# Contraction-outermost order behind the norms, late squares, and SSD decay masks as scaled ScalarE copies

## The chip, the cores and the metric

The kernel runs on one core of a Trainium2 chip: TensorE (PE, matrix products), VectorE (DVE), ScalarE (ACT), GpSimd (POOL) and SyncE (SP, which issues the DMAs). The metric is the device time of one launch in microseconds (us), taken as the median of several runs.

## The reference

The function is one inference step of a two-layer recurrent trunk of width 1024 over 592 columns (16 meta tokens, 512 prompt tokens, 8 samples of 8 tokens). Layer 0 mixes with SSD heads (16 heads of 64) and RG-LRU blocks, layer 1 with GLA and HGRN heads. Each layer ends twice in a layer norm:

```
h = LN(alpha*h + mixer(h));  h = LN(alpha*h + relu(h @ w1)^2 @ w2)
LN(x): mu = mean(x); var = mean((x - mu)^2); (x - mu) * rsqrt(var + eps) * g + b

# SSD, per chunk of q tokens and per head
xbc = silu(b + sum(full[:, t:t+L] * w[t] for t in range(4)))     # causal convolution of width 4
b = cumsum(log_a);  decay = exp(where(t >= s, b_t - b_s, -inf))  # q x q, per head
y_intra = (c_t . b_s) * decay @ (x*dt);  y_inter = (c_t . S) * exp(b_t)
S = S * exp(b_last) + b^T (x * dt * exp(b_last - b))
```

All of it is float32; new recurrent states are outputs too.

## The kernel before, in words

Activations lie with the 1024 features in eight tiles of 128 partitions and with the 592 columns along the free dimension, in two halves of 296 (288 in the later stages, where the meta columns are dropped). A product of float32 quality is three fp32r matmuls (high·high, high·low, low·high), so one output tile of one half is 24 matmuls of 128x128x296: eight contraction steps k times three. Weights arrive by DMA as units of 128x1024 (`raw`); ACT casts the high part (L126) and DVE subtracts the low part (L127). Five units of prepared weights and five PSUM banks `pm` are in rotation (three more banks, `px`, serve small products).

A task (`Task`, L276) is one weight unit over both halves; `mm` (L176) runs its 24 matmuls of one half, and `consume` empties the bank. `run(..., by_half=True)` goes through all tasks' first halves, then through their second halves. `later` holds work that `mm` issues after a given k. The order of every engine comes from a scheduler that looks at the whole program with its own costs; each engine then runs its list strictly in order.

**The norms** (`Norm`, L395) stand behind each output projection and each MLP. While the last product is made, each finished residual tile is added to a running sum (L444) and its square (ACT, L446) to a running sum of squares (DVE, L447). `finishing` (L457) sends both sums through PE with a matrix of ones (L463 mean, L465 variance), and then, tile by tile, DVE and POOL subtract the mean (L478, L480), DVE scales (L494), ACT rounds to the high part of the next input `h` (L495) and DVE makes the low part (L496). For half 0 the statistics are issued inside the first product of half 1, after step `FIK`; for half 1 they come after it. The next stage's first block of products (in the MLP L648, `w1` tasks; in the odd mixer a small product `lr` at L247 and q, k, v) starts on half 0 while half 1 is being finished. Its banks are emptied by ACT (L588 in the MLP, L1366 and L1381 in the odd mixer).

**The SSD part** works in two groups of four pairs of heads (`pair`, L832), in stages between which other work is woven. A pair needs the log decays (high and low part, `lah` and `lal`, 128 x 16 heads per chunk) times a triangular mask: `rr` (2 x 4 chunks x 2 heads x 128) and `rx` (2 x 2 x 80). POOL makes them with two 128x1024 products (L843) and two of 128x160 (L845). PE sums them (L879, L884), ACT takes the exponential (L881, L885), DVE multiplies it by the scores (L886, L887). Then come the state products: DVE L897 writes `yi0` from a `px` bank, which PE's L918 waits for; L911 updates the running state `S`, which L925 reads; POOL's L899 scales the samples' states `sin`. Between these, `conv_task` (L687) makes the next inputs: ACT empties the bank (L697 to L702), DVE does the first tap (L706, tensor_scalar) and the next taps (L708 twice, L781 once), ACT the silu (L783), DVE L787 the product. The same `conv_task` serves the RG-LRU blocks, whose PE product is L1067.

Of the kernel before, what the change touches and what calls it, by code (L numbers as in the profile page):

```python
# [8 lines left out]
F32 = mybir.dt.float32  # L9
# [5 lines left out]
P = 128  # L15
# [8 lines left out]
NPM = 5  # L24
NB = 5
SHK = 5
FIK = 3
FINY = (2, 4, 6)
SUBP = (1, 3, 5, 7)
KS = 8 - NB  # L30
# [41 lines left out]
def _trunk(ctx, tc, nc, I, O):  # L72
# [12 lines left out]
    def pm():  # L85
        return pmp.tile([P, 512], F32, tag="pm", name="pm")
# [83 lines left out]
    def next_unit():  # L170
        u = state["use"]
        state["use"] += 1
        prep_to(u + 1 + LOOK)
        return prepped.pop(u)
# [25 lines left out]
    def flush():  # L200
        while pending:
            pending.pop(0)()
# [66 lines left out]
    def drain():  # L269
        while active or later:  # L270
            for k in sorted(later):
                for fn in later.pop(k):
                    fn()
            weave()

    class Task:  # L276
# [6 lines left out]
        def half(self, i):  # L283
# [8 lines left out]
            flush()  # L292
            weave()

    def run(tasks, by_half=False, after=None):
        if by_half:
            for i in range(2):
                for t in tasks:
                    t.half(i)
                if after:  # L300
                    after(i)
        else:
            for t in tasks:
                t.half(0)
                t.half(1)
# [89 lines left out]
    class Norm:  # L395
# [3 lines left out]
        def __init__(self, new, rs, halves, gname, bname, layer, final=False):  # L399
            self.rs, self.halves, self.final = rs, halves, final  # L400
            self.gname, self.bname, self.layer = gname, bname, layer
            self.new = new

        def shift(self):

# [25 lines left out]
        def add(self, k, i):  # L431

            c0, c1 = self.halves[i]
            r = self.rs[k][:, c0:c1]
            if k == KS:
                V.tensor_tensor(r, r, self.c[:, c0:c1], OP.subtract)
            s, ss = self.s[:, c0:c1], self.ss[:, c0:c1]
            if k == 0:
                A.activation(ss, r, AF.Square)
                return  # L440
            if k == 1:
                G.tensor_tensor(s, self.rs[0][:, c0:c1], r, OP.add)
            else:
                (V if k == KT - 1 else G).tensor_tensor(s, s, r, OP.add)  # L444
            q = self.t[k % 2][:, c0:c1]
            A.activation(q, r, AF.Square)  # L446
            V.tensor_tensor(ss, ss, q, OP.add)  # L447

        def finish(self, i, dst):
            if i == 0:  # L450
                later.setdefault(FIK, []).append(lambda: step(self.finishing(i, dst)))
            else:
                drain()
                for _ in self.finishing(i, dst):
                    pass

        def finishing(self, i, dst):  # L457
            c0, c1 = self.halves[i]
            n = c1 - c0
            gname, bname, layer = self.gname, self.bname, self.layer  # L460
            s, ss, rstd, m2 = (t[:, c0:c1] for t in (self.s, self.ss, self.rstd, self.m2))
            mu = px()[:, :n]
            PE.matmul(mu, ones, s, start=True, stop=True)  # L463
            var = px()[:, :n]
            PE.matmul(var, ones, ss, start=True, stop=True)  # L465
            A.activation(m2, mu, AF.Square, scale=1.0 / D)
            if ln_set:
                tc.keep_in_program_order(A.preload_act_table_set("natural_log_exp_and_others"))
                ln_set.clear()
            V.scalar_tensor_tensor(rstd, var, 1.0 / D, m2, OP.mult, OP.subtract)  # L470
            A.activation(rstd, rstd, AF.Ln, bias=LN_EPS)
            A.activation(rstd, rstd, AF.Exp, scale=-0.5)
            mn = self.t[0][:, c0:c1]
            A.activation(mn, mu, AF.Copy, scale=1.0 / D)
            for k in range(KT):
                r = self.rs[k][:, c0:c1]
                if k not in SUBP:
                    V.tensor_tensor(r, r, mn, OP.subtract)  # L478
                else:
                    G.tensor_tensor(r, r, mn, OP.subtract)  # L480
            for k in range(KT):
                if k in FINY:
                    yield
                r = self.rs[k][:, c0:c1]
                gain, b = vc(gname, layer * 8 + k), vc(bname, layer * 8 + k)
                if self.final:
                    if k % 2 == 0:
                        y = act_tile(hp, "h").bitcast(F32)[:, :, 0:n]
                    V.scalar_tensor_tensor(r, r, gain, rstd, OP.mult, OP.mult)
                    A.activation(y[:, k % 2], r, AF.Identity, bias=b)  # L490
                    if k % 2:
                        nc.sync.dma_start(O["yT"][:, k - 1:k + 1, c0 - NM:c1 - NM], y)
                else:
                    V.scalar_tensor_tensor(r, r, gain, rstd, OP.mult, OP.mult)  # L494
                    A.activation(dst[k][:, 0, c0:c1], r, AF.Identity, bias=b)  # L495
                    V.scalar_tensor_tensor(dst[k][:, 1, c0:c1], r, b, dst[k][:, 0, c0:c1].bitcast(F32),  # L496
                                           OP.add, OP.subtract)
# [49 lines left out]
    def mlp(H, layer, halves, last, keep=None):  # L547
# [3 lines left out]
        with ExitStack() as st:  # L551
# [93 lines left out]
                        G.tensor_scalar(rs[k], rs[k], vc("ln2b", layer * 8 + k), None, OP.add)  # L645
                        G.dma_start(keep[:, k], rs[k])

            run([w1(0, f) for f in W1_ORDER[:4]], by_half=True)  # L648
            for k, f in enumerate(W1_ORDER[4:]):
                run([w1(0, f)])  # L650
                residual(2 * k)
# [24 lines left out]
    def even_mixer(H, g):  # L676
# [10 lines left out]
        def conv_task(i, w, b, done):  # L687
# [3 lines left out]
            def consume(p, c0, c1, half):  # L691
# [11 lines left out]
                G.tensor_copy(pconv[:, i], t[:, 528:531])  # L703
                G.tensor_copy(sconv[:, i], s8(t)[:, :, 8:11])
                acc = cp.tile([P, PW], F32, tag="acc", name="acc")
                V.tensor_scalar(acc[:, 0:OW], t[:, 0:OW], w(0), b, OP.mult, OP.add)  # L706
                for k in (1, 2):
                    V.scalar_tensor_tensor(acc[:, 0:OW], t[:, k:k + OW], w(k), acc[:, 0:OW], OP.mult, OP.add)  # L708
                done(t, acc)
# [122 lines left out]
        def pair(j, xs, zs, gs):  # L832
# [6 lines left out]
            nc.sync.dma_start(sin, I["sst"][j])  # L839
            rr = s1.tile([P, 2, 4, 2, P], F32R, tag="rr", name="rr")  # L840
            rx = s1.tile([P, 2, 2, 80], F32R, tag="rx", name="rx")
            for i, l in enumerate((lah.bitcast(F32), lal.bitcast(F32))):
                G.tensor_tensor(rr[:, i], l[:, 1:5, hh].unsqueeze(3).to_broadcast([P, 4, 2, P]),  # L843
                                umask[:, None, None, :].to_broadcast([P, 4, 2, P]), OP.mult)
                G.tensor_tensor(rx[:, i], l[:, 0, hh].unsqueeze(2).to_broadcast([P, 2, 80]),  # L845
                                uxmask[:, None, 0:80].to_broadcast([P, 2, 80]), OP.mult)
            xr = s1.tile([P, 2, 3, 40], F32, tag="xr", name="xr")
            A.copy(xr, xs[:, 0:80].rearrange("p (h c) -> p h c", h=2).unsqueeze(2).to_broadcast([P, 2, 3, 40]))
            yield
            xd = s2.tile([P, 5, 2, 64], F32, tag="xd", name="xd")  # L850
            xdte = s1.tile([P, 4, 2, 64], F32, tag="xdte", name="xdte")
            xst = s1.tile([P, 2, 2, 64], F32, tag="xst", name="xst")
# [268 lines left out]
    def odd_mixer(H, g):  # L1121
# [278 lines left out]
        for h in range(4):  # L1400
            q, k, v0, v1 = (g(n) for n in ("q", "k", "v", "v"))
            tasks = [copy_task(q, TAIL), copy_task(k, FULL), copy_task(v0, FULL), copy_task(v1, FULL)]
            if h == 0:
                run([Task(H, FULL, lr_consume, small=wsr[:, 1])] + tasks[0:NB], by_half=True)
                run(tasks[NB:])
            else:
                run(tasks)
            z = [g("zs"), g("zs")]
# [214 lines left out]
```

## Time and profile before

| | us |
|---|---|
| median of 3 runs (lowest, highest) | 1928.42 (1928.1, 1928.71) |
| profiled execution | 1926.06 |
| its span, first to last instruction | 1924.3 |
| mean granted TensorE clock in the span | 0.987 of full |
| PE busy | 1858.2 (97%) |
| DVE busy | 1297.1 (67%) |
| ACT busy | 886.0 (46%) |
| POOL busy | 417.2 (22%) |

PE is busy for 97% of the span, so the time can fall only where PE waits or where its granted clock is low. The profile names for each wait of PE the instruction that ended it.

### The profile page before, as it was taken

What the parts mean: (1) busy time and instruction counts of PE and PEld (TensorE: products, weight loads), DVE (VectorE), ACT (ScalarE), POOL (GpSimd) and SP (SyncE); (2) the same over time, 40 slices, a digit from 0 to 9 for tenths busy, and PEclk for the clock granted to TensorE, in tenths of its full rate; (3) what the DMA queues carried; (4) which work ended last, traced back from release to release, by engine and by line L of the source; (5) the groups of instructions that cost most, each with busy time, mean ns of one, the idle gap of its engine ahead of it and who ended that gap; (6) DMA issues with size and microseconds to landing.
All of it is one profiled execution on the core that took longest, in us unless ns stands there. A gap on an engine that the chain in (4) does not pass through costs nothing.

```text
span 1924.3 us, 33593 instructions
## 1 busy us (share of the span) xinstructions
PE 1858.2 (97%) x13854; PEld 1819.0 (95%) x13854; DVE 1297.1 (67%) x2035; ACT 886.0 (46%) x1550; POOL 417.2 (22%) x435
## 2 busy tenths in 40 slices
PE   8998899999999999998999999999999999999996
PEld 8998799899999999998999999999999999999996
DVE  7997766877975756549645465665755976666647
ACT  5333246623644444324644455665732653534333
POOL 2554432214100000035422222221203200000024
PEclk9999899999999999999999999999999999999998
DMA  6232221421213131322332233223231214141311
GB/s 205 91 114 72 75 100 47 132 88 47 87 56 120 46 127 48 122 76 72 132 113 104 100 104 106 84 90 102 91 126 56 77 56 132 46 131 55 122 55 50
DMA packets 68761, 175.97 MB, mean 91 GB/s; under 512 B 6624, under 2 KB 30304, under 8 KB 67456
## 3 DMA queue, kind: packets, MB, share of 16 engines
q1 hardware_dynamic: 67968, 171.40, 26.5%
q8 instruction: 109, 1.79, 0.4%
q0 software_dynamic: 640, 2.43, 0.4%
q14 instruction: 44, 0.36, 0.1%
HBM read 154.54 MB, written 19.25 MB: 90 GB/s over the span
## 4 chain that ended last, share of the span: by engine, by line
PE 80%; DVE 13%; ACT 3%; issue 3%; POOL 0%; DMA 0%; SPq 0%; ACTq 0%; DVEq 0%; POOLq 0%
PE pm L182 55%; PE pm L195 14%; DVE w L127 1%; DVE r L424 1%; DVE h L496 1%; DVE r L494 1%; PE px L1326 1%; DVE r L478 1%; PE px L1337 1%; PE px L1336 1%; PE px L1067 1%; DVE lnq L447 1%; DVE acc L708 1%; PE px L925 1%; DVE ln L447 1%
## 5 line engine op out<-in xcount | busy, mean ns | idle before, releaser
L182 PE MATMUL pm<-h,w 128*128 128x296 f32 (+2 forms) x8256 | 1178.2, 301 | 11.0 <-ACT h L308 5.4
L182 PEld LDWEIGHTS pm<-h,w 128*128 128x128 f32 x8256 | 1132.6, 189 | 22.6 <-ACT h L308 5.4
L127 DVE TENSOR_TENSOR w<-raw,w 128x1024 fp32r<-128x1024 f32 (+1 forms) x300 | 369.7, 1233 | 165.1 <-ACT w L126 164.5
L126 ACT CAST w<-raw 128x1024 fp32r<-128x1024 f32 (+1 forms) x300 | 304.2, 1015 | 301.6 <-PE pm L195 152.2
L195 PE MATMUL pm<-ff,w 128*128 128x296 f32 (+1 forms) x2016 | 273.3, 297 | 0.0
L195 PEld LDWEIGHTS pm<-ff,w 128*128 128x128 f32 x2016 | 271.9, 188 | 0.1
L620 POOL TENSOR_TENSOR sq<-sq 128x296 f32<-128x296 f32 (+1 forms) x32 | 21.5, 674 | 651.4 <-ACT sq L618 651.4
L182 PE MATMUL pm<-m,w 128*128 128x296 f32 (+1 forms) x768 | 108.2, 304 | 0.0
L182 PE MATMUL pm<-ff,w 128*128 128x296 f32 (+1 forms) x768 | 108.0, 303 | 0.0
L182 PEld LDWEIGHTS pm<-m,w 128*128 128x128 f32 x768 | 106.8, 194 | 0.8 <-issue 0.3
L182 PEld LDWEIGHTS pm<-ff,w 128*128 128x128 f32 x768 | 106.6, 193 | 0.8 <-issue 0.3
L607 DVE TENSOR_TENSOR ff<-sq,ff 128x888 fp32r<-128x888 f32 (+3 forms) x48 | 58.4, 1221 | 42.1 <-ACT ff L606 42.1
L588 ACT ACTIVATE sq<-pm 128x296 f32<-128x296 f32 (+1 forms) x96 | 37.9, 414 | 87.0 <-PE pm L182 66.0
L606 ACT CAST ff<-sq 128x888 fp32r<-128x888 f32 (+3 forms) x48 | 50.3, 1050 | 39.6 <-DVE sq L601 38.9
L1361 POOL TENSOR_TENSOR o<-o,zs 128x576 f32<-128x576 f32 x16 | 31.3, 1967 | 148.7 <-DVE o L1360 148.7
L1280 POOL TENSOR_TENSOR sin<-sin,ebl 128x1024 f32<-128x1024 f32 (+1 forms) x12 | 35.8, 2980 | 106.1 <-issue 101.2
L211 DVE TENSOR_TENSOR r<-r,pm 128x296 f32<-128x296 f32 (+1 forms) x96 | 43.5, 453 | 18.6 <-PE pm L195 18.0
L589 ACT ACTIVATE sq<-sq 128x296 f32<-128x296 f32 (+1 forms) x96 | 41.2, 450 | 0.8
L1366 ACT COPY v<-pm 128x296 f32<-128x296 f32 x32 | 12.9, 405 | 58.6 <-PE pm L182 58.6
L214 DVE TENSOR_TENSOR r<-r,pm 128x296 f32<-128x296 f32 (+1 forms) x72 | 32.6, 452 | 10.2 <-PE pm L195 10.2
L618 ACT ACTIVATE sq<-pm 128x296 f32<-128x296 f32 (+1 forms) x32 | 13.0, 414 | 56.8 <-PE pm L182 53.8
L495 ACT ACTIVATE h<-r,vec 128x296 fp32r<-128x296 f32 (+1 forms) x48 | 23.8, 536 | 31.5 <-DVE r L494 31.5
(390 smaller groups left out, 2261.3 us busy)
## 6 DMA issues: line engine op xcount, KB each, us to landing
raw<-in_w_dram SPq DMA_DIRECT2D x252, 512.0 KB, 3.3
sin<-in_sst_dram SPq DMA_DIRECT2D x8, 512.0 KB, 3.7
out_ssd_s_dram<-sin SPq DMA_DIRECT2D x8, 512.0 KB, 3.1
sin<-in_gst_dram SPq DMA_DIRECT2D x4, 1024.0 KB, 5.7
out_gla_s_dram<-sin SPq DMA_DIRECT2D x4, 1024.0 KB, 3.9
sin<-in_hst_dram SPq DMA_DIRECT2D x8, 512.0 KB, 4.4
out_hgrn_s_dram<-sin SPq DMA_DIRECT2D x8, 512.0 KB, 3.5
xt<-in_x_dram SPq DMA_DIRECT2D x16, 148.0 KB, 4.2
```

What stands on the lines that cost most here:

```text
L126: A.copy(w[:, 0, :n], r)
L127: V.tensor_tensor(w[:, 1, :n], r, w[:, 0, :n].bitcast(F32), OP.subtract)
L182: PE.matmul(p[:, :n], w[:, a, ks], xs[k][:, b, c0:c1], start=(k == 0 and i == 0), stop=(k == KT - 1 and i == 2))
L195: PE.matmul(p[:, :n], w[:, a, ks], xs[k][:, b, :n], start=(first and k == 0 and i == 0), stop=(k == 3 and i == 2), skip_group_check=True)
L211: V.tensor_tensor(y, y, p[:, :n], OP.add)
L214: V.tensor_tensor(y, y, p[:, :n], OP.subtract)
L447: V.tensor_tensor(ss, ss, q, OP.add)
L588: A.activation(q, p, AF.Relu)
L589: A.activation(q, q, AF.Square)
L606: A.copy(t[:, 0, a:e, :n], s[:, a + 1:e + 1, :n])
L607: V.tensor_tensor(t[:, 1, a:e, :n], s[:, a + 1:e + 1, :n], t[:, 0, a:e, :n].bitcast(F32), OP.subtract)
L1280: G.tensor_tensor(sin, sin, ebl[:, 0:8].unsqueeze(2).to_broadcast([P, 8, N]), OP.mult)
```

## The change

The statistics of half 0 are issued after step 6 instead of step 3 of the first product of half 1. `together` runs several tasks with the contraction step outermost: step k of all tasks, then step k+1, and empties all banks at the end. It is used for the first four tasks behind the three norms that have a successor (four tasks on half 0, then two and two on half 1). The addition of a square to its running sum is issued one tile later. Weights of four units are asked for before the drain. The first convolution tap becomes an ACT instruction, and the masks times log decays become 20 ACT copies per pair of heads, each with a per-partition scale.

```diff
-FIK = 3
+FIK = 6
+    def together(tasks, i):
+        ps = []
+        for t in tasks:
+            if t.small is None and t.w is None:
+                t.w = next_unit()
+            ps.append(pm())
+        for k in range(KT):
+            ks = slice(k * P, (k + 1) * P)
+            for t, p in zip(tasks, ps):
+                c0, c1 = t.halves[i]
+                if t.small is not None:
+                    ops = [(p[:32], t.small[:, k, :], b) for b in range(2)]
+                else:
+                    ops = [(p, t.w[:, a, ks], b) for a, b in ((0, 0), (0, 1), (1, 0))]
+                for j, (o, w, b) in enumerate(ops):
+                    PE.matmul(o[:, :c1 - c0], w, t.xs[k][:, b, c0:c1], start=(k == 0 and j == 0),
+                              stop=(k == KT - 1 and j == len(ops) - 1))
+            for fn in later.pop(k, ()):
+                fn()
+        for t, p in zip(tasks, ps):
+            c0, c1 = t.halves[i]
+            t.consume(p[:32 if t.small is not None else P, :c1 - c0], c0, c1, i)
+            flush()
+            weave()
...
             A.activation(q, r, AF.Square)
-            V.tensor_tensor(ss, ss, q, OP.add)
+            self.add_square()
+            self.square = (ss, q)
+        def add_square(self):
+            if self.square:
+                ss, q = self.square
+                V.tensor_tensor(ss, ss, q, OP.add)
+            self.square = None
...
             else:
+                prep_to(state["use"] + 4)
                 drain()
...
         def finishing(self, i, dst):
+            self.add_square()
...
-            run([w1(0, f) for f in W1_ORDER[:4]], by_half=True)
+            ts = [w1(0, f) for f in W1_ORDER[:4]]
+            together(ts, 0)
+            together(ts[:2], 1)
+            together(ts[2:], 1)
...
-                V.tensor_scalar(acc[:, 0:OW], t[:, 0:OW], w(0), b, OP.mult, OP.add)
+                A.activation(acc[:, 0:OW], t[:, 0:OW], AF.Identity, scale=w(0), bias=b)
...
-            for i, l in enumerate((lah.bitcast(F32), lal.bitcast(F32))):
-                G.tensor_tensor(rr[:, i], l[:, 1:5, hh].unsqueeze(3).to_broadcast([P, 4, 2, P]),
-                                umask[:, None, None, :].to_broadcast([P, 4, 2, P]), OP.mult)
-                G.tensor_tensor(rx[:, i], l[:, 0, hh].unsqueeze(2).to_broadcast([P, 2, 80]),
-                                uxmask[:, None, 0:80].to_broadcast([P, 2, 80]), OP.mult)
+            def decays(m):
+                for i, l in enumerate((lah.bitcast(F32), lal.bitcast(F32))):
+                    for h in range(2):
+                        def scaled(out, mask, c):
+                            A.activation(out, mask, AF.Copy, scale=l[:, c, 2 * j + h:2 * j + h + 1])
+                        if m == 2:
+                            scaled(rx[:, i, h], uxmask[:, 0:80], 0)
+                        else:
+                            for c in (2 * m, 2 * m + 1):
+                                scaled(rr[:, i, c, h], umask, c + 1)
+            decays(0)
...
             yield
+            decays(1)
+            decays(2)
...
             if h == 0:
-                run([Task(H, FULL, lr_consume, small=wsr[:, 1])] + tasks[0:NB], by_half=True)
-                run(tasks[NB:])
+                ts = [Task(H, FULL, lr_consume, small=wsr[:, 1])] + tasks
+                together(ts[:4], 0)
+                ts[4].half(0)
+                together(ts[:2], 1)
+                together(ts[2:4], 1)
+                ts[4].half(1)
```

In the changed file the lines below L291 lie further down: L843 becomes L888, L899 becomes L950, L463 and L465 become L500 and L502, L783 becomes L823, and so on.

POOL's list in the sixth pair of heads (pair 5), before: `lah` and `lal` are the log decays, `msk` the triangular mask.

```order
L868 TENSOR_TENSOR xdte<-xd,ex 128x512
L703 COPY pconv<-pad 128x3
L843 TENSOR_TENSOR rr<-lah,msk 128x1024
L845 TENSOR_TENSOR rx<-lah,msk 128x160
L843 TENSOR_TENSOR rr<-lal,msk 128x1024
L845 TENSOR_TENSOR rx<-lal,msk 128x160
L899 TENSOR_TENSOR sin<-sin,ex 128x1024
```

Four mask products stand between the copy of the convolution state and the scaling of `sin`. POOL's list at the same place after the change:

```order
L744 COPY sconv<-pad 128x24
L1003 TENSOR_TENSOR y<-y,zs 128x592
L919 TENSOR_TENSOR xdte<-xd,ex 128x512
L743 COPY pconv<-pad 128x3
L950 TENSOR_TENSOR sin<-sin,ex 128x1024
L735 MEMSET pad 128x3
```

The four products have left POOL's list; the scaling of `sin` follows the copy directly.

ACT's list in the same pair, before (`de` and `dx` are the exponentials, `pad` and `acc` belong to the convolution):

```order
L871 CAST xsr<-xst 120x256
L702 COPY pad<-pm 128x296
L126 CAST w<-raw 128x1024
L881 ACTIVATE de<-px 128x512 x2
L885 ACTIVATE dx<-px 128x160
L783 ACTIVATE pad<-acc 128x616
```

The silu of the convolution (L783) follows the exponentials directly, and the first tap is not in ACT's list. ACT's list at the same place after the change:

```order
L922 CAST xsr<-xst 120x256
L742 COPY pad<-pm 128x296
L126 CAST w<-raw 128x1024
L746 ACTIVATE acc<-pad,hcb,hcw 128x616
L932 ACTIVATE de<-px 128x512 x2
L936 ACTIVATE dx<-px 128x160
L888 ACTIVATE rr<-msk,lah 128x128 x4
L888 ACTIVATE rr<-msk,lal 128x128 x4
L888 ACTIVATE rr<-msk,lah 128x128 x3
L823 ACTIVATE pad<-acc 128x616
```

Eleven of the next pair's twenty copies stand ahead of the silu, and the first tap stands ahead of the exponentials.

PE's list behind the first norm, around the statistics of half 1, before (`pm_5260` and `pm_5294` are banks of the first two `w1` tasks, `h_4996` to `h_5003` the eight input tiles):

```order
L182 MATMUL pm_5260<-h_5001,w_4896 128x296 x3
L182 MATMUL pm_5260<-h_5002,w_4896 128x296 x3
L182 MATMUL pm_5260<-h_5003,w_4896 128x296 x3
L182 MATMUL pm_5294<-h_4996,w_4930 128x296
L463 MATMUL px_5192<-lns_4790,ones_78 128x296
L465 MATMUL px_5194<-lnq_4791,ones_78 128x296
L182 MATMUL pm_5294<-h_4996,w_4930 128x296 x2
```

The statistics stand behind all 24 matmuls of the first task and one of the second. PE's list at the same place after the change (`h_5123` to `h_5130` are the eight input tiles, the banks are those of four tasks):

```order
L311 MATMUL pm_5388<-h_5125,w_5023 128x296 x3
L311 MATMUL pm_5394<-h_5125,w_5057 128x296 x3
L311 MATMUL pm_5400<-h_5125,w_5091 128x296 x3
L311 MATMUL pm_5388<-h_5126,w_5023 128x296 x3
L500 MATMUL px_5325<-lns_4918,ones_78 128x296
L311 MATMUL pm_5394<-h_5126,w_5057 128x296 x3
L311 MATMUL pm_5400<-h_5126,w_5091 128x296 x2
L311 MATMUL pm_5406<-h_5123,w_5321 128x296
L311 MATMUL pm_5406<-h_5124,w_5321 128x296
L502 MATMUL px_5327<-lnq_4919,ones_78 128x296
```

The statistics of half 1 have moved from behind 25 matmuls of the new stage, which read all eight tiles of `h`, to behind 32, which read the first four.

## Rows read from the trace of the kernel before

**Rows 1.** The page's part 1, busy time of each engine, share, instructions
```profile
PE 1858.2 (97%) x13854; PEld 1819.0 (95%) x13854; DVE 1297.1 (67%) x2035; ACT 886.0 (46%) x1550; POOL 417.2 (22%) x435
```
**Rows 2.** Waits of PE, whole span: instruction, releaser, us in total, times, longest
```profile
PE px L918 <- DVE yi L897: 9.8, 3, 4.9
PE px L463 <- DVE ln L444: 8.2, 3, 3.5
PE px L463 <- DVE lns L444: 6.9, 2, 3.5
...
PE px L925 <- DVE S L911: 4.6, 3, 2.2
PE pm L182 <- DVE h L496: 3.0, 4, 1.1
PE px L1067 <- DVE xr L1055: 2.8, 1, 2.8
...
PE px L822 <- DVE bmx L820: 1.9, 1, 1.9
PE pm L247 <- DVE h L496: 1.7, 2, 1.3
PE pm L182 <- ACT h L495: 1.6, 2, 0.8
PE px L818 <- ACT btok L815: 1.5, 1, 1.5
```
**Rows 3.** Stretches: us, PE busy (matmuls), granted clock, DMA share, GB/s
```profile
170.00:176.00 6.00, 4.30 (x19) 0.50 0.04 12
200.00:204.00 4.00, 3.31 (x16) 0.57 0.15 38
228.00:234.00 6.00, 5.84 (x25) 0.50 0.54 163
463.00:469.00 6.00, 5.38 (x18) 0.50 0.01 3
876.00:879.00 3.00, 3.00 (x11) 0.50 0.02 5
1890.00:1896.00 6.00, 5.19 (x17) 0.50 0.00 0
```
**Rows 4.** Timeline of DVE in pair 5: start, us, instruction
```profile
186.09 0.60 DVE L706 TENSOR_SCALAR acc<-pad,hcw,hcb 128x616 f32<-128x616 f32 x1 [0.77 <-ACT pad L702]
...
190.56 2.50 DVE L708 SCALAR_TENSOR_TENSOR acc<-pad,hcw,acc 128x616 f32<-128x616 f32 x1
...
197.04 0.28 DVE L897 TENSOR_TENSOR yi<-px,ex 128x128 f32<-128x128 f32 x1
```
**Rows 5.** Timeline of POOL in pair 5
```profile
189.52 2.88 POOL L843 TENSOR_TENSOR rr<-lal,msk 128x1024 fp32r<-128x1024 f32 x1
...
193.33 2.89 POOL L899 TENSOR_TENSOR sin<-sin,ex 128x1024 f32<-128x1024 f32 x1
```
**Rows 6.** Groups of DVE by line, 55 to 150 us: busy us, mean ns
```profile
L708 DVE SCALAR_TENSOR_TENSOR acc<-pad,hcw,acc 128x616 f32<-128x616 f32 x10 | 8.5, 852 | 0.0
```
**Rows 7.** Timeline of ACT, pairs 4 and 5; idle time before an instruction in brackets
```profile
179.21 0.17 ACT L697 COPY pad<-pm 128x16 f32<-128x16 f32 x1 [8.45 <-PE pm L182]
...
185.65 0.41 ACT L702 COPY pad<-pm 128x296 f32<-128x296 f32 x1 [0.84 <-PE pm L182]
...
196.97 0.72 ACT L783 ACTIVATE pad<-acc 128x616 f32<-128x616 f32 x1 [8.79 <-DVE acc L781]
```
**Rows 8.** Timeline of PE at the first norm
```profile
463.62 1.35 PE L463 MATMUL px<-lns,ones 128*128 128x296 f32 x2 [3.48 <-DVE lns L444]
...
489.33 10.84 PE L182 MATMUL pm<-h,w 128*128 128x296 f32 x76
```
**Rows 9.** Timeline of DVE at the first norm
```profile
487.94 0.45 DVE L444 TENSOR_TENSOR lns<-lns,r 128x296 f32<-128x296 f32 x1
```
**Rows 10.** The page's part 5, L127: busy us, mean ns, idle before
```profile
L127 DVE TENSOR_TENSOR w<-raw,w 128x1024 fp32r<-128x1024 f32 (+1 forms) x300 | 369.7, 1233 | 165.1 <-ACT w L126 164.5
```

More of the change, by code (lines that the diff above doesn't have):

```diff
@@ L446, in add @@
             A.activation(q, r, AF.Square)
-            V.tensor_tensor(ss, ss, q, OP.add)
+            self.add_square()
[4 more added lines that the diff above has]
+                V.tensor_tensor(ss, ss, q, OP.add)
+            self.square = None
         def finish(self, i, dst):
```

## The prediction

> **What bounds the kernel now.** The page's first part comes first: PE is busy for 97% of the span [rows 1], so only its waits and its half-clock stretches can be won. The list of PE's waits comes second [rows 2]. The reader is to see that nearly all releasers there are DVE: in the SSD part L918 waits 9.8 us in three pieces for DVE's L897 and L925 4.6 us in three for L911; at the norms L463 waits 8.2 + 6.9 = 15.1 us for the last sum (four waits of about 3.5 and one of 1.2 at the very end), and the first products behind three norms wait 3.0 + 1.6 + 1.7 = 6.3 us for tiles of `h`. The table of stretches comes third [rows 3]: behind such waits the granted clock is 0.50, the lower of the two levels (1.2 instead of 2.4 GHz). What that costs is half of PE's busy time there: 2.15, 1.4 and 2.9 us in the SSD part (6.5 together; at 0.57 I take 0.43 of 3.31), and 2.7, 1.5 and 2.6 us at three of the four norms. The third norm shows the same wait and I take 1.5 there too, so 8.3 at the four. Last come the timelines of one SSD pair [rows 4, 5, 7] and of one norm [rows 8, 9].
>
> **SSD pairs.** Pair 5 shows why DVE is late. L708 takes 0.85 us where POOL is quiet [rows 6] and 2.50 while POOL multiplies masks [rows 4, 5]; three such instructions (L708 twice, L781) stand in the chain to L897. POOL suffers too: its mask product takes 2.88 there. The change takes away the masks and L706 (0.60): 3 x 1.65 + 0.60 = 5.55 us. POOL's L899 stays (2.89) and can still stretch one of the three, so 3.9 us are sure in a pair. Pairs 5 and 6 share the 4.9 us of L918 that the longest wait (4.9, pair 4) leaves, 2.45 each: gone. The remaining 1.45 us come off L925's wait of 2.2, in two pairs: 2.9. In pair 4 two other groups of DVE instructions lie beside the masks; I take 4.3 of its 4.9, between 3.3 (L899 stretches one more) and 4.9. Waits: 4.9 + 2.9 + 4.3 = 12.1 us. Of the 6.5 us at the lower clock I take half, 3.3, since 0.7 us of wait stays in each of the later pairs: 15.4 us, between 7 (only L706 and half of the contention) and 20.8 (all L918 waits, two of L925, all of the clock).
>
> On the contention the Trainium skill ("SBUF — State Buffer", section "Who interferes with whom") says that DVE and GpSimd hold the shared ports exclusively for a whole instruction, so the later one waits until the other ends, and that ScalarE waits for nobody. By that rule L899 can hold up a pair by its full 2.89 us instead of 1.65, and the SSD term would be some 2.5 us lower; the trace has both engines slow at once (2.50 against 0.85 and 2.88), so I keep 1.65.
>
> The copies go to ACT: 20 per pair. No copy of 128x128 from SBUF is in these rows; the nearest are 0.17 us for 128x16 and 0.41 for 128x296 [rows 7], from PSUM. I take 0.27, by width: 5.4 us per pair, between 3.4 and 8.2. A copy below 0.17 would change nothing. What hides them: ACT stands idle 8.79 us before the silu of pair 5 and 8.45 us before the next emptying of a bank [rows 7]. Eleven copies stand ahead of that silu (3.0 us, at most 4.5), nine behind it, ahead of a weight cast. Behind them wait the silu, the emptying of a bank for `zs`, and the cast, with DVE and PE behind those; in both gaps they fit twice. The first tap costs ACT 0.72, as the silu of the same width does [rows 7]; it stands behind L702, on which DVE's L706 waited as well, but also behind a weight cast, so L708 starts up to a microsecond later than L706 ended, in time that the chain has just gained: nothing.
>
> **Start.** L818 and L822 wait 1.5 + 1.9 us [rows 2] on ACT and DVE work that loses the contention and L706. The new copies and taps on ACT delay the small chain of constants before it. I take half, 1.7 (0 to 3.4).
>
> **RG-LRU.** L1067 waits 2.8 us [rows 2] behind a chain with one L706 in it: 0.6, and half of the about 1.5 us of low clock that follows such a wait: 1.3 (0 to 4.3).
>
> **Norms, what goes.** From the group at the first norm a matmul costs 10.84/76 = 0.143 us [rows 8]. Nine more of them ahead of the first statistics cut each of the four 3.5 us waits by 1.3: 5.2. The 2.2 that stay are of the size of single SSD waits, and 1.9 (L822) was followed by no fall of the clock while 2.8 was, so I take the 8.3 us of low clock as gone but for 0.8: 7.5. Contraction-outermost asks for a new tile of `h` every 12 matmuls (1.7 us) instead of every 3 (0.4), so the 6.3 us of waits for `h` in half 0 go. The late squares move single additions of 0.45 us beside each other on DVE: nothing. Together 19.0.
>
> **Norms, what comes.** With nothing to wait for, PE arrives early at the statistics of half 1, and DVE is then late: at the first norm DVE ends the last sum at 487.94 + 0.45 = 488.39 [rows 9]. In the new order one L127 (1.23 us [rows 10]) of the three before it stands ahead of the first statistics, in idle time: 487.2. PE leaves the first statistics at 463.6 plus about 0.9, then runs 99 matmuls of half 1 and 32 of the new stage: 464.5 + 131 x 0.143 = 483.2. A wait of 4.0, between 2 and 5.5. I take 3.0 at the second and third norm, where the sums end nearer to PE's arrival: 10.0. The final norm has no next stage; its 1.2 stays. Second, a bank: the four tasks of half 0 hold four of five `pm` banks, and the first is emptied by ACT (L588) behind all eight roundings of half 1 (L495). The first task of half 1 runs in the fifth bank alone up to step 5, then the second must wait. Nothing in the trace is that wait; the nearest are the 0.8 us waits for L495 [rows 2], plus an emptying of 0.41 [rows 7]: 1.2 at three norms, 3.6, between 0 and 2.5 each. Third, the clock: three waits of 3 to 4 us are followed by the lower level; with 1.5 us each, as at the second norm [rows 3], and one spared by chance: 3.5. The weights of the fourth task are needed after 8 matmuls instead of 72; ACT casts them before that in its list and DVE's part is needed only behind the statistics: nothing. Together 17.1. The norms win 19.0 - 17.1 = 1.9 us (-7 to +14), nearly all at the final one.
>
> **The sum.** 15.4 + 1.7 + 1.3 + 1.9 = 20.3 us, from the profiled 1926.06: 1905.8. The median of the runs is 2.4 above the profiled execution, so I forecast 1908.
>
> **Rivals.** (A) DVE is not late at the second statistics: freed of the wait for PE at the half clock, it ends its sums some 3 us sooner. For it: DVE idles between the first statistics and its next work in the present order. Against: behind that it is busy without a gap. It would give back two thirds of 17.1: 1897. (B) The new waits at three norms are 5.5 and each bank wait 2.5, each with a fall of the clock: (1.5 + 2.5 + 2.0) less than reckoned at the first norm, half of that at the others, some 10 us: 1918. For it: DVE's list between the two statistics is as long as before but for one L127; against: the first task fills 17 matmuls meanwhile. (C) The contention is not the masks' but that of all of POOL's work: then only L706 and one stretched instruction per pair go, the SSD term is 4 and the time 1919. Against: L708 takes 0.85 or 2.50 in these rows, nothing between. (D) Slower than before: ACT becomes the bound of the SSD pairs. The eleven copies ahead of the silu are covered by 8.79 us and the nine behind it by 8.45, so it decides from 0.8 us per copy. At 1.0 the silu is late by 11 - 8.8 = 2.2 us, and with it L787, L911 and PE's L925, and the cast and the bank behind the nine are late by 0.6: 2.8 us in each of eight pairs, 22, while of the sum only RG-LRU and the norms are won (3.2): 1947. Against: a copy of 128x296 takes 0.41 [rows 7].
>
> **How the numbers follow.** Forecast 0.54, A 0.17, B 0.15, C 0.07, D 0.07. The forecast's own bounds with half of the norms' and the SSD's spread are 1899 to 1915; A and B widen that to 1896 and 1920, and what is left out is D, part of C and of A. A measurement of this kernel can tell about 0.2% (4 us) from no change. Slower than that is D, 0.07; within it the tail of B and C, 0.04; faster 0.89.
>
> **What would show it.** In the changed profile: L708 and L781 near 0.85 in pairs 4 to 6 with at most one stretched; no wait of L918 over 1 us; copies of 0.2 to 0.4 us; the first wait for the last sum near 2.2 at each norm without a stretch at 0.50; a second wait of 2 to 5 us behind the first three norms with a stretch at 0.50 after it; no waits for `h` in half 0; a matmul of the second task waiting for ACT in half 1. The prediction is wrong if POOL's L899 alone keeps DVE slow, if the clock falls at the 2.2 us waits as well, or if the second waits do not come.

## The result and the profile after

The changed kernel takes 1906.03 us (median of 4 runs, 1903.47 to 1907.38) against 1928.26 of the kernel before beside it: a ratio of 0.9885, 95% interval 0.9868 to 0.9902, 22.2 us less. Forecast were 1908, range 1896 to 1920. The profiled execution took 1907.38, with a span of 1905.6 (before 1924.3: 18.7 less). It is the slowest of the four, and that of the kernel before (1926.06) is one of its faster ones, so the places below add up to 18.7 and not to 22.2 us.

The first line of the page's part 1 answers to [rows 1]. The reader is to see that POOL and DVE lost 50 and 34 us of work and ACT won 58. PE has the same number of matmuls; it is busy for 5.1 us less, at a mean granted clock of 0.990 instead of 0.987, and stands idle for 52.5 instead of 66.1 us of the span.

```profile
PE 1853.1 (97%) x13854; PEld 1814.4 (95%) x13854; DVE 1263.0 (66%) x2015; ACT 944.3 (50%) x1730; POOL 366.9 (19%) x403
```

PE's waits over the whole span answer to [rows 2] (instruction, releaser, us in total, times, longest).

```profile
PE pm L311 <- DVE r L556: 6.4, 5, 1.8
...
PE px L500 <- DVE ln L471: 4.4, 3, 1.5
PE pm L311 <- DVE r L671: 3.8, 2, 2.4
PE px L500 <- DVE lns L471: 3.0, 2, 1.5
PE px L1118 <- DVE xr L1106: 2.6, 1, 2.6
PE px L969 <- DVE yi L948: 2.5, 1, 2.5
PE px L976 <- DVE S L962: 2.4, 2, 1.2
...
PE pm L311 <- ACT sq L625: 1.7, 2, 1.4
PE pm L311 <- ACT lgf L1432: 1.1, 1, 1.1
```

L969 (L918 before) fell from 9.8 to 2.5 us, L500 (L463) from 15.1 to 7.4, and the waits for `h` are gone but for one of 0.47 us. New are 6.4 + 3.8 = 10.2 us of L311, the first products behind a norm, and 0.9 us at L908 in three pieces.

Where the time went is best read by comparing the start of the same PE instruction in the two traces. The lead of the changed kernel, in us:

| place | lead |
|---|---|
| pair 0, transposed outputs (L940, now L991) | 3.2 |
| first transposes of pair 4 (L857, now L908) | 0.5 |
| L940 of pairs 4, 5, 6 | 1.8, 6.6, 13.2 |
| end of RG-LRU (last L1067) | 13.2 |
| first L1247 (now L1298) behind the second norm | 13.3 |
| small product ahead of the last norm (L421, now L448) | 13.1 |
| statistics of half 1 at the last norm | 17.5 |
| last instruction | 18.7 |

So the start won 3.2, pairs 0 to 3 lost 2.7, the next three won 12.7, RG-LRU and the first three norms nothing net, and the last norm and what follows it 5.6.

DVE in pairs 5 and 6 answers to [rows 4] (start, us, instruction). The taps run at 0.85 us again, L948 (L897 before) comes at 191.82 instead of 197.04 (1.8 us of this was the lead at pair 4), and POOL's L950, the one 128x1024 product left, holds up one instruction per pair: L938 takes 2.04 in pair 5, L821 2.52 in pair 6. The rows of POOL's L950 stand below those of DVE.

```profile
186.41 0.85 DVE L748 SCALAR_TENSOR_TENSOR acc<-pad,hcw,acc 128x616 f32<-128x616 f32 x1
...
189.09 2.04 DVE L938 TENSOR_TENSOR dx<-dx,cbx 128x160 f32<-128x160 f32 x1
191.05 0.85 DVE L821 SCALAR_TENSOR_TENSOR acc<-pad,hcw,acc 128x616 f32<-128x616 f32 x1
191.82 0.28 DVE L948 TENSOR_TENSOR yi<-px,ex 128x128 f32<-128x128 f32 x1
...
211.72 2.52 DVE L821 SCALAR_TENSOR_TENSOR acc<-pad,hcw,acc 128x616 f32<-128x616 f32 x1
```

```profile
188.95 1.99 POOL L950 TENSOR_TENSOR sin<-sin,ex 128x1024 f32<-128x1024 f32 x1 [4.41 <-PE px L945]
...
211.35 2.23 POOL L950 TENSOR_TENSOR sin<-sin,ex 128x1024 f32<-128x1024 f32 x1 [4.17 <-PE px L945]
```

ACT in pair 5 answers to [rows 7]. Four copies take 1.29 us, about 0.3 each, and the silu L823 still waits for DVE, not DVE for it.

```profile
187.08 1.29 ACT L888 ACTIVATE rr<-msk,lah 128x128 fp32r<-128x128 f32 x4
...
192.02 0.72 ACT L823 ACTIVATE pad<-acc 128x616 f32<-128x616 f32 x1 [1.61 <-DVE acc L821]
```

PE at the first norm answers to [rows 8]. The first statistics wait 1.50 us instead of 3.48. Then 14 matmuls of the new stage run with two waits for L556, which empties the banks of the stage before; L500 at 474.05 does not wait.

```profile
449.65 0.77 PE L500 MATMUL px<-lns,ones 128*128 128x296 f32 x2 [1.50 <-DVE lns L471]
...
467.00 1.32 PE L311 MATMUL pm<-h,w 128*128 128x296 f32 x8 [1.60 <-DVE r L556]
470.08 4.13 PE L311 MATMUL pm<-h,w 128*128 128x296 f32 x18 [1.75 <-DVE r L556]
474.05 0.66 PE L500 MATMUL px<-lns,ones 128*128 128x296 f32 x2
...
487.82 11.06 PE L311 MATMUL pm<-h,w 128*128 128x296 f32 x79 [1.35 <-ACT sq L625]
```

The clock answers to [rows 3] (stretch: us, PE busy, granted clock, DMA share, GB/s). It stays full behind the first statistics (449 to 455 and 1877 to 1883; before 0.50) and falls behind the new waits.

```profile
170.00:176.00 6.00, 6.00 (x27) 0.50 0.27 100
336.00:340.00 4.00, 3.97 (x15) 0.59 0.37 131
449.00:455.00 6.00, 5.34 (x36) 1.00 0.01 4
470.00:474.00 4.00, 3.92 (x18) 0.59 0.00 0
880.00:887.00 7.00, 6.31 (x26) 0.55 0.21 75
1494.00:1500.00 6.00, 4.73 (x20) 0.50 0.00 0
1877.00:1883.00 6.00, 6.00 (x42) 1.00 0.00 0
```

### The profile page after: what moved, and what is told of

Read it like the earlier page. It is cut to its first block, busy times and chain, and to the rows that moved or that the text cites. A ratio compares the mean times of both kernels' runs of the same rounds, so it can differ in the third digit from the quotient of the medians.

```text
span 1905.6 us, 33734 instructions
## 1 busy us (share of the span) xinstructions
PE 1853.1 (97%) x13854; PEld 1814.4 (95%) x13854; DVE 1263.0 (66%) x2015; ACT 944.3 (50%) x1730; POOL 366.9 (19%) x403
## 3 DMA queue, kind: packets, MB, share of 16 engines
q8 instruction: 109, 1.79, 0.4%
q0 software_dynamic: 640, 2.43, 0.3%
## 4 chain that ended last, share of the span: by engine, by line
PE 79%; DVE 14%; ACT 4%; issue 3%; POOL 0%; DMA 0%; SPq 0%; ACTq 0%; DVEq 0%
PE pm L182 52%; PE pm L195 14%; PE pm L311 2%; DVE w L127 2%; DVE r L515 1%; DVE r L531 1%; DVE h L533 1%; DVE r L451 1%; PE px L1377 1%; DVE acc L748 1%; ACT w L126 1%; PE px L1388 1%; PE px L1387 1%; PE px L1118 1%; PE px L1317 1%
## 5 line engine op out<-in xcount | busy, mean ns | idle before, releaser
L182 PE MATMUL pm<-h,w 128*128 128x296 f32 (+2 forms) x7728 | 1103.9, 301 | 6.4 <-ACT h L334 5.5
L127 DVE TENSOR_TENSOR w<-raw,w 128x1024 fp32r<-128x1024 f32 (+1 forms) x300 | 367.2, 1225 | 184.0 <-ACT w L126 183.2
L311 PE MATMUL pm<-h,w 128*128 128x296 f32 (+1 forms) x528 | 83.4, 315 | 12.7 <-DVE r L556 6.4
L311 PEld LDWEIGHTS pm<-h,w 128*128 128x128 f32 x528 | 77.9, 201 | 17.2 <-ACT h L532 12.0
L211 DVE TENSOR_TENSOR r<-r,pm 128x296 f32<-128x296 f32 (+1 forms) x96 | 43.5, 453 | 18.8 <-PE pm L195 18.1
L655 ACT ACTIVATE sq<-pm 128x296 f32<-128x296 f32 (+1 forms) x32 | 13.1, 415 | 56.8 <-PE pm L182 53.8
```

The costliest lines, as they stand in the source:

```text
L127: V.tensor_tensor(w[:, 1, :n], r, w[:, 0, :n].bitcast(F32), OP.subtract)
L182: PE.matmul(p[:, :n], w[:, a, ks], xs[k][:, b, c0:c1], start=(k == 0 and i == 0), stop=(k == KT - 1 and i == 2))
L211: V.tensor_tensor(y, y, p[:, :n], OP.add)
L311: PE.matmul(o[:, :c1 - c0], w, t.xs[k][:, b, c0:c1], start=(k == 0 and j == 0), stop=(k == KT - 1 and j == len(ops) - 1))
```

## The experiments

Times are medians beside runs of the kernel before on the same chip.

**The two parts apart.** The first is the kernel before with masks and tap on ACT, the second the kernel before with the norm part. Only the lines that tell them apart are shown; "..." marks what is left out.

```diff
-V.tensor_scalar(acc[:, 0:OW], t[:, 0:OW], w(0), b, OP.mult, OP.add)
+A.activation(acc[:, 0:OW], t[:, 0:OW], AF.Identity, scale=w(0), bias=b)
...
-G.tensor_tensor(rr[:, i], ...)
-G.tensor_tensor(rx[:, i], ...)
+decays(0)
...
+decays(1)
+decays(2)
```

```diff
-FIK = 3
+FIK = 6
...
-V.tensor_tensor(ss, ss, q, OP.add)
+self.add_square()
...
+prep_to(state["use"] + 4)
...
-run([w1(0, f) for f in W1_ORDER[:4]], by_half=True)
+together(ts, 0)
+together(ts[:2], 1)
+together(ts[2:], 1)
...
```

> The kernel before with the SSD part of the change alone (masks as ACT copies, first tap on ACT), norms untouched. Theory 1 (the changed kernel's gain of 22.2 us is 13.2 us won up to the end of the SSD part, nothing net at the first three norms, and 5.5 us at the last norm and behind it; the parts simply add): about 1928.3 - 13.2 = 1915, with the four pairs of the first group 0.75 us longer each than before and the waits of L918 gone in the two later pairs. Rival (the norms' order carries the gain through a clock that no longer falls at their first statistics, SSD half or less of it): 1920 or more.

> The kernel before with the norm part alone (statistics of half 0 after step 6, contraction outermost, late squares, weights asked for before the drain); masks on POOL and first tap on DVE as before. Theory 1 (additive): 1928.3 - 5.5 = 1923, all of it behind the last MLP; at the first three norms the first statistics wait 1.5 instead of 3.5 us, and 3 to 4 us of waiting come back at the first products behind the norm, which need four banks that DVE has not emptied yet. Rival (norms carry the gain): 1915 or less.

Measured: 1913.39 against 1928.58 (ratio 0.9916, 0.9900 to 0.9932), and 1919.39 (0.9960, 0.9947 to 0.9973). That is 15.2 and 9.2 us, 24.4 together against 22.2 for the whole; by the spans (1911.6 and 1917.2 against 1924.3) 12.7 and 7.1, 19.8 together against 18.7. The parts add within the scatter of the runs, and the SSD part carries more. The norm part alone won 3.7 us more by the medians than theory 1 said, 1.6 more by the spans. The waits are those of the whole: first statistics at 1.5, L311 at 1.6 and 1.7. By the start of the same instructions the last norm and what follows won 5.6 us, as in the whole; the other 1.5 were won at the third norm, where the granted clock stays at 1.00 in this execution (1506 to 1512 us) and is 0.50 in that of the changed kernel (1494 to 1500), behind nearly the same waits (1.57 and 1.57 us, there 1.56 and 1.27): chance and not order.

```profile
462.94 0.77 PE L500 MATMUL px<-lns,ones 128*128 128x296 f32 x2 [1.51 <-DVE lns L471]
...
480.29 1.33 PE L311 MATMUL pm<-h,w 128*128 128x296 f32 x8 [1.60 <-DVE r L556]
483.37 4.23 PE L311 MATMUL pm<-h,w 128*128 128x296 f32 x18 [1.74 <-DVE r L556]
```

**The tap.** On ACT the tap stands behind the weight cast. ACT's rows of pair 2, the third, in the changed kernel, then DVE's of the kernel before: from the bank's emptying L742 at 113.06 to the tap's end at 115.22 it is 2.16 us, before, with L702 at 114.77, the tap ends at 115.81, after 1.04 us.

```profile
113.06 0.41 ACT L742 COPY pad<-pm 128x296 f32<-128x296 f32 x1 [0.84 <-PE pm L182]
113.36 1.05 ACT L126 CAST w<-raw 128x1024 fp32r<-128x1024 f32 x1
114.31 0.91 ACT L746 ACTIVATE acc<-pad,hcb,hcw 128x616 f32<-128x616 f32 x1
```

```profile
115.21 0.60 DVE L706 TENSOR_SCALAR acc<-pad,hcw,hcb 128x616 f32<-128x616 f32 x1 [0.46 <-ACT pad L702]
```

Three kernels ask for it: the changed one with the tap on DVE, the kernel before with the masks alone, and the kernel before with the tap alone.

```diff
-A.activation(acc[:, 0:OW], t[:, 0:OW], AF.Identity, scale=w(0), bias=b)
+V.tensor_scalar(acc[:, 0:OW], t[:, 0:OW], w(0), b, OP.mult, OP.add)
```

> The changed kernel with the first convolution tap back on DVE; masks stay on ACT. Theory 1 (the 0.75 us that each of the pairs 0 to 3 lost come from the tap, which on ACT stands behind the weight cast and starts 1.1 us later than on DVE): these pairs are as long as before (21.0 us instead of 21.75), 3 us won there; in pairs 5 and 6 DVE has 0.6 us more and L925's counterpart waits that much longer, 1 us lost: 1904. Rival (the twenty copies in ACT's list make the silu late): pairs 0 to 3 stay at 21.75 us and the time is 1906 to 1908.

> The kernel before with the masks on ACT and nothing else. Theory 1 (the masks alone make the SSD gain: 18.9 us up to the end of the SSD part in the run with the tap on DVE): 1928.9 - 18.9 = 1910, below the run that has the tap on ACT as well (1913.4). Rival (tap and masks both contribute, as the prediction reckoned with 0.6 us per pair): above 1913.

> The kernel before with the first tap on ACT and nothing else; masks stay on POOL. Theory 1 (on ACT the tap stands behind the weight cast: 0.75 us lost in each of the pairs 0 to 3, at most 0.6 won back in each of the pairs 4 to 6, where the contention still sets the time): 1929 to 1931. Rival (0.6 us less on DVE in every chain): 1926 to 1927.

Measured: 1902.69 (0.9866, 0.9853 to 0.9880); 1910.59 against 1926.64 (0.9908, 0.9893 to 0.9923); 1929.43 against 1926.64 (1.0010, 1.0002 to 1.0019). PE's rows of the second and third pair show it without scatter: 21.77 us from one to the next in the changed kernel, 21.03 with the tap on DVE, 21.02 with the masks alone, 21.74 with the tap alone (before: 21.02). First the changed kernel, then these three in the same order.

```profile
96.18 0.34 PE L991 MATMUL px<-msk,yi 128*128 128x80 f32 x2
...
117.95 0.34 PE L991 MATMUL px<-msk,yi 128*128 128x80 f32 x2
```

```profile
94.83 0.34 PE L991 MATMUL px<-msk,yi 128*128 128x80 f32 x2
...
115.86 0.34 PE L991 MATMUL px<-msk,yi 128*128 128x80 f32 x2
```

```profile
96.14 0.34 PE L950 MATMUL px<-msk,yi 128*128 128x80 f32 x2
...
117.16 0.34 PE L950 MATMUL px<-msk,yi 128*128 128x80 f32 x2
```

```profile
96.98 0.34 PE L940 MATMUL px<-msk,yi 128*128 128x80 f32 x2
...
118.72 0.34 PE L940 MATMUL px<-msk,yi 128*128 128x80 f32 x2
```

So the tap loses 0.75 us in each of the first pairs, with or without the copies, and the copies lose nothing there. The masks alone make the SSD gain; the tap takes about 3 us of it. The loss of 1 us that theory 1 saw in pairs 5 and 6 with the tap on DVE did not come, rather the reverse: from pair 4 to 5 and from 5 to 6 it is 21.3 and 22.3 us with the tap on DVE and 22.4 and 22.3 with it on ACT. So the later tap costs 1.1 us between pairs 4 and 5 as well: PE's wait of 1.23 us at L976 in pair 5 is there only with the tap on ACT. The rows show a likely reason. In the changed kernel L938 starts 0.14 us behind POOL's L950 and is held up (189.09 and 188.95 above); with the tap on DVE the chain is early enough that L821 starts 0.17 us ahead of L950, and POOL is held up instead:

```profile
184.14 0.85 DVE L821 SCALAR_TENSOR_TENSOR acc<-pad,hcw,acc 128x616 f32<-128x616 f32 x1
```

```profile
184.31 2.70 POOL L950 TENSOR_TENSOR sin<-sin,ex 128x1024 f32<-128x1024 f32 x1 [4.41 <-PE px L945]
```

The tap on ACT ahead of the weight cast was not tried.

**The banks behind a norm.** Half 0 of the new stage two tasks at a time, so that two banks are asked for instead of four.

```diff
-together(ts, 0)
+together(ts[:2], 0)
+together(ts[2:], 0)
...
-together(ts[:4], 0)
+together(ts[:2], 0)
+together(ts[2:4], 0)
```

> The changed kernel with half 0 of the first block behind a norm taken two tasks and two tasks at a time instead of four, so that the new stage starts with two banks instead of four. Theory 1 (the waits of 3.4, 3.8 and 3.0 us at the first products behind three norms look like waits for a bank, but the bank is late because DVE's list is late as a whole): the waits move from the first products to the statistics of half 1 or to the tiles of h, about 2 to 3.5 us at each norm, and the time is 1904 to 1907. Rival (the number of banks asked for at once is the cause): the waits go without a successor, with their stretches of low clock, some 3 us at each of three norms: 1896 to 1899.

Measured: 1903.70 (0.9871, 0.9858 to 0.9885), theory 1 but for 0.3 us. PE at the first norm: 32 matmuls run through, and L500 waits 4.00 us where L311 had waited 1.60 + 1.75.

```profile
461.69 4.66 PE L311 MATMUL pm<-h,w 128*128 128x296 f32 x32
470.35 1.22 PE L500 MATMUL px<-lns,ones 128*128 128x296 f32 x2 [4.00 <-DVE lns L471]
```

DVE's last sum shows why. First the changed kernel, then two tasks at a time: it ends at 472.88 and at 470.29, in both 23.2 us behind the start of the first statistics (449.65 and 447.06), however many banks PE asks for.

```profile
472.43 0.45 DVE L471 TENSOR_TENSOR lns<-lns,r 128x296 f32<-128x296 f32 x1
```

```profile
469.84 0.45 DVE L471 TENSOR_TENSOR lns<-lns,r 128x296 f32<-128x296 f32 x1
```

The wait moves and hardly shrinks: 4.00, 4.12 and 3.81 us at L500 for 3.35, 3.8 and 3.0 at L311, and L311's later waits for ACT fall from 1.7 + 1.1 to 0.9. Of the 2.3 us of lead won at the first two norms about half is the clock, which comes back sooner behind the second norm in this execution (0.76 from 880 to 887 us, in the changed kernel 0.55).

**DVE's list.** The changed kernel without DVE's subtraction of the mean at the first three norms.

```diff
 if k not in SUBP:
-    V.tensor_tensor(r, r, mn, OP.subtract)
+    if self.final:
+        V.tensor_tensor(r, r, mn, OP.subtract)
```

> The changed kernel without DVE's subtraction of the mean (four of eight tiles, both halves) at the first three norms; this leaves out part of the computation there. Theory 1 (the waits of 3.4, 3.8 and 3.0 us behind these norms come from the length of DVE's list, of which these subtractions are about 4 us per half): the waits behind the norms shrink to under 1 us and their stretches of low clock go: 1906 - 10 - 3 = about 1893. Rival (four banks asked for at once): the waits stay above 2 us each and the time is above 1901.

Measured: 1899.77 (0.9845, 0.9830 to 0.9860), between the two. DVE's last sum at the first norm ends at 468.33, 21.2 us behind the first statistics (447.14) instead of 23.2, so the list does set that distance. But it got only 2.0 us shorter for some 4 us of subtractions, and the waits stay above 2 us, as the rival said: 2.86, 1.99 + 1.56 and 2.79 us at the three norms.

```profile
467.88 0.45 DVE L471 TENSOR_TENSOR lns<-lns,r 128x296 f32<-128x296 f32 x1
```

```profile
466.28 2.61 PE L311 MATMUL pm<-h,w 128*128 128x296 f32 x12 [2.86 <-DVE r L557]
```

Of the lead of this execution on that of the changed kernel 2.6 us were there at the end of RG-LRU, ahead of the first norm, where the two kernels have the same instructions. Leaving instructions out also reorders the lists, so this shows the direction and not that DVE's list is the whole cause.

**The step of the statistics and the late squares.**

```diff
-FIK = 6
+FIK = 3
```

```diff
-self.add_square()
-self.square = (ss, q)
+V.tensor_tensor(ss, ss, q, OP.add)
```

> The changed kernel with the statistics of half 0 back behind step 3. Theory 1 (at the first three norms DVE's list sets the end, so PE waits 1.3 us more at the statistics and 1.3 less behind the norm; only at the last norm, where nothing follows, does it cost 1.3, and the clock falls there again, 2.6): 1907 to 1910. Rival (each of the four waits and falls of the clock comes back in full, 1.3 + 2 each): 1916 to 1920.

> The changed kernel with each square added at once instead of one tile later. Theory 1 (DVE's two waits of 0.5 us for ACT's square stood in the chain to the last sum at the first statistics, 3.5 us with the step alone would have become 2.2 and is 1.5 with the late squares): the first statistics wait 2.2 again at all four norms, which costs 0.7 at the last one and at most that at the others: 1907 to 1909. Rival (late squares do nothing): 1906, waits of 1.5.

Measured: 1909.89 (0.9899, 0.9881 to 0.9917) and 1907.92 (0.9893, 0.9876 to 0.9909), both theory 1 by the time, though both intervals overlap that of the changed kernel; the waits are what tells them apart. With step 3 the first statistics wait 2.7, with the squares at once 2.27, 2.65, 2.28 and 2.29 at the four norms: step and squares took 1.2 and 0.8 us off the 3.5. With step 3 the last norm has its fall of the clock again (1.33 us for the two matmuls that take 0.75 in the changed kernel), and with the squares at once too (1.08):

```profile
1879.40 1.33 PE L500 MATMUL px<-ln,ones 128*128 128x288 f32 x2 [2.72 <-DVE ln L471]
```

```profile
1874.33 1.08 PE L499 MATMUL px<-ln,ones 128*128 128x288 f32 x2 [2.29 <-DVE ln L471]
```

**Both edits, and three matmuls more.** The tap on DVE and two tasks at a time together, as above; then the same with the statistics of half 0 later:

```diff
-FIK = 6
+FIK = 7
```

> The changed kernel with both edits: first tap on DVE, and half 0 two tasks at a time. Theory 1 (the edits act at different places, the tap in the SSD part, the grouping at the first two norms, where it won 2.4 us): 1902.7 - 2.4 = 1900. Rival (what the grouping won is the clock's chance and not the order): 1902 to 1904.

> The kernel with both edits (tap on DVE, two tasks at a time) and the statistics of half 0 three matmuls later, behind step 7. Theory 1 (the wait at the first statistics falls from 1.5 to 1.1 us, and only the last norm can keep that, since behind the other three DVE's list sets the end): 1901.0 - 0.4, within 1900 to 1901. Rival (all four norms keep 0.4): 1899.

Measured: 1901.00 against 1929.21 (0.9853, 0.9839 to 0.9868) and 1899.56 against 1926.64 (0.9854, 0.9841 to 0.9868). The two edits add; both kernels beat the changed one. By their ratios step 7 and step 6 do not differ. The waits do: the first statistics wait 1.10, 1.12, 0.98 and 1.12 us instead of 1.52 to 1.54, and those of half 1 behind the first three norms 3.58, 4.02 and 3.36 instead of 3.99, 4.12 and 3.81. So no norm gives the 0.4 us back, as the rival said and theory 1 did not; in the time it cannot be told from the scatter.

## Why the prediction was right, point by point

- **What bounds the kernel**: right. PE stood idle for 13.6 us less and was busy for 5.1 us less with the same matmuls, together the 18.7.
- **SSD pairs, masks**: right in kind: L748 and L821 at 0.85, one instruction of the chain held up by L950 per pair, L969 and L976 down from 14.4 to 4.9 us. 12.7 us were measured in pairs 4 to 6, 15.4 forecast. The waits were mis-sized: pair 4 kept 2.49 us where 0.6 was forecast, against the sign that no wait of L918 would be over 1 us (what holds it was not tried), L976 kept 1.23 and 1.18 where 0.76 each was. Of the low clock about half stayed, as forecast, but all of it in one place, behind pair 4, and by chance (last section).
- **SSD pairs, copies**: 0.3 us each with neighbours overlapped, about 0.4 alone, against 0.27; hidden, as reckoned.
- **SSD pairs, tap**: the step that failed. "It stands behind L702 ... but also behind a weight cast ... in time that the chain has just gained: nothing" is not what came. In pairs 0 to 3 DVE had no contention in that part of its chain ([rows 6] is from there), so nothing was gained to hide it: 0.75 us a pair, 2.7 in all. Between pairs 4 and 5 it cost 1.1 us more, where the chain now comes just behind POOL's L950. L706's 0.60 us, counted as won, was a loss.
- **Start**: 3.2 instead of 1.7: both waits go nearly whole, and each part takes away one of them. With the masks alone L818 still waits 1.45 us and L822 no longer does; with the tap alone L822 still waits 1.79 and L818 only 0.39. (The leads, 2.6 and 2.3, say less: in the run with the tap alone 0.9 us of it is there after the first product, which no edit touches.)
- **RG-LRU**: nothing instead of 1.3: the wait is 2.6 instead of 2.8 and the clock still falls behind it (0.59 from 336 to 340 us; in the run with the squares at once it stays at 1.00 behind the same wait).
- **First statistics**: 1.5 instead of 2.2 us, since the late squares, costed at nothing, are worth 0.8. The clock stays full there, as forecast, but not for the reason given: with the squares at once the waits are those of the forecast, 2.27 to 2.65 us, and the clock falls behind two of the four. So that it stayed full at all four is owed in part to the term put at nothing.
- **Waits for `h` in half 0**: gone, as forecast.
- **Second statistics**: a wait of 4.0, 3 and 3 us was forecast at L500; 3.35, 3.8 and 3.0 came (1.60 + 1.75, 1.34 + 2.43, 0.17 + 1.56 + 1.27), but at L311, for banks that DVE empties late. The size was right, the place was not: that the new stage asks for four banks at its first step was missed. With two banks the wait stood at L500 with 4.00. The low clock came with it, as forecast.
- **Bank in half 1**: 1.35, 1.08 and 0.33 us (and 0.47 for a rounding of `h` at the third norm) against 1.2 each.
- **Sum**: of the first three norms nothing net, as forecast; the last norm and the end 5.6 instead of about 4. The errors cancel: 2.7 short by the tap in pairs 0 to 3, 2.7 in pairs 4 to 6, 1.3 in RG-LRU, against 1.5 at the start and 3.6 at the norms. 18.7 by the profiled executions, 20.3 forecast; 22.2 by the medians. That the sum came so near is luck: the terms miss by 1.3 to 3.6 us each.
- **Rivals**: A falls, for DVE is late at the second statistics (PE waits 4.00 us there once two banks suffice); C falls with the taps at 0.85, and D with the copies hidden. The waits of B came in size, 3 to 4 us, but not at 5.5.

On the contention the value kept, 1.65 us, was right, and the reason was not. The prediction reads 2.50 and 2.88 us as both engines being slow at once; the rows show each waiting for the other to end. DVE's L708 ends 0.66 us behind POOL's L843 before the change (193.06 and 192.40, [rows 4, 5]), L821 0.66 us behind L950 after it (214.24 and 213.58), L938, which takes 0.31 us alone, 0.19 us behind L950 (191.13 and 190.94). Part of POOL's 2.88 us is a wait as well: that L843 starts at 189.52 inside DVE's L127, which runs until 190.64, while the one that starts just ahead of DVE's L708 (186.73) takes 1.91 us:

```profile
189.17 1.47 DVE L127 TENSOR_TENSOR w<-raw,w 128x1024 fp32r<-128x1024 f32 x1
```

```profile
186.68 1.91 POOL L843 TENSOR_TENSOR rr<-lah,msk 128x1024 fp32r<-128x1024 f32 x1 [0.37 <-PE px L884]
```

So the trace agrees with the rule that the prediction quotes from the Trainium skill ("SBUF — State Buffer", section "Who interferes with whom") and sets aside: the later instruction waits until the other ends. So L899 could not have held a pair up by its 2.89 us, which hold a wait of POOL's own; L950 has 1.86 and 1.85 us left when L821 and L938 start, and they take 1.67 and 1.73 us longer than alone.

## What to carry to other kernels

Work that leaves an engine is worth what it held up there, and what it costs on the new engine is its place in that list: 0.6 us moved off DVE lost 0.75 per pair in pairs 0 to 3, behind a cast of 1.05 us on ACT. An order that asks for inputs later asks for more output banks sooner; here neither moved the end of the stage, which was set by the engine that both makes the inputs and empties the banks. Compare the start of the same instruction in two traces, place by place: gains and losses of 3 us each that cancel in the total are seen at once.

## What the runs showed of the hardware

The same wait is not always followed by the same fall of the clock. In pair 4 PE waits 2.49 us in the changed kernel and the granted clock is 0.50, the lower of its two levels, from 170 to 176 us (above). With the squares at once, the instructions are the same up to there, and so is the wait, but the clock stays at 1.00:

```profile
168.76 1.11 PE L968 MATMUL px<-xsr,bmx 120*128 120x128 f32 x8 [2.49 <-DVE yi L947]
```

```profile
170.00:176.00 6.00, 5.90 (x58) 1.00 0.43 138
```

Half of the 6.00 us that PE is busy at 0.50 in the changed kernel is 3.0 us, most of the scatter of that kernel's runs (3.9 us).

Shorter waits are no safe side either. The prediction took it that waits of 1.9 and 2.2 us leave the clock alone. With the squares at once the waits of 2.27 and 2.28 us at the first and third norm do, and behind those of 2.65 and 2.29 us at the second and the last the clock is 0.72 on the mean of six us (857 to 863 and 1874 to 1880). At L1298 PE waits 1.93 us in the changed kernel, and the clock stays at 1.00 (1375 to 1379); with two tasks at a time the same instruction waits 1.94 us, and the clock is 0.58 behind it (1371 to 1375). Waits of 1.5 us at the first statistics were followed by 1.00 at all four norms of the changed kernel. What decides it was not tried.
